# Hybrid S5 and sparse-attention layer on one core: modulation and gate rows on TensorE, attention from unsplit q and k with its division moved to the product with v, elementwise stages in place in PSUM

## The chip, the cores and the metric

The kernel runs on one core of one Trainium2 chip. Its time is the device time of one execution in microseconds. The engines are TensorE (PE, matmuls; PEld is its weight load), VectorE (DVE), ScalarE (ACT), GpSimd (POOL) and SyncE (SP, which issues the DMAs here). Each takes its instructions strictly in the order in which the program gives them, and waits on semaphores for the others.

## What is computed

One layer for a sequence of 512 tokens of width 1024:

```
mod = silu(c) @ w_ada + b_ada                    # 3 x 1024: shift, scale, gate
h = rms_norm(x, g) * (1 + scale) + shift
proj = h @ w_in                                  # 1024 x 3656, then split
y_ssm  = s5(u) with a GLU, * silu(z)             # 32 groups x 16 channels, 64 complex states each
score  = sum_h w_idx * relu(q_idx k_idx^T)       # causal; the 128 best keys of each query stay
logits = (rms_norm(q) rms_norm(k)^T) / 8 + bias  # 8 heads x 64, -inf where a key was not picked
y_attn = (softmax(logits) @ v) * silu(z')
x = x + gate * (concat(y_ssm, y_attn) @ w_out)
```

## The kernel before

Nothing in this kernel is issued where it is written. `record` writes every operation into a list, under a stage name and with the engines that could do it; `Plan.schedule` then makes one order for each engine, by a table of due times per stage (`STAGES`), of shifts per tile (`SHIFT`), of allowed engines (`ONLY`) and by estimated costs (`_cost`). Line 418 issues all of them, so every row of the profile has that line, and tiles are told apart by name. SBUF tiles come from pools of numbered slots (`SLOTS`: 65 of 512 columns, 4 for raw weights, 8 for their converted halves) and PSUM from 8 banks of 128 x 512 fp32.

The large products are split: a weight `wr` is copied to fp32r `wh` and the remainder becomes `wl` (helpers `hi`, `lo`); the same for the activations, and `mm3` adds three fp32r matmuls.

What the change touches, in program order:

- **Modulation** (stages mod0 to mod4, five blocks of 1, 1, 2, 2, 2 groups of 128 channels). The row `modrow` = silu(c) @ w_ada comes for blocks 0 and 1 from matmuls into `pm` (the vector, padded to 32 columns, `cpad`, is the stationary operand, and the eight parts of the sum go to four groups of 32 output rows), and for the blocks in `SIDE` = (2, 3, 4) from VectorE, which multiplies each loaded `wa` (128 x 512) by one column of `cpad` and adds: eight instructions for a block. Then come `Ac`, `Bc`, `hf`, `hh`, `hl`, and the matmuls `pi` of the first 640 columns of w_in.
- **Indexer and top-k** (rel, topk). For each of three query tiles and eight heads two matmuls into `pr`, a relu into `rl`, a multiply-add into `acc`; then 16 rounds of max and match_replace for three tiles (`m`, `work`), which give `mask1` to `mask3`.
- **SSM** (`ssm_quad`, four times). Two PSUM tiles `pd` are copied to `Dt`; six elementwise products and sums, two scans, and six more on 128 x 512, on VectorE or GpSimd, lead to `Xr`, `Xi`, then the matmuls `py` and 16 Gelu pieces `zt`.
- **Projections** (`pp`, 128 x 512, 24 matmuls each).
- **Attention** (at0 to at3, two heads each, four query tiles of widths 128 to 512). `pbx` spreads the norms, `qk` is scaled, and q and k are split into `qs`, `ks`, `kl` (ten half-height operations for each head pair). Logits `pl` come from two fp32r matmuls; bias `G` plus mask is added on VectorE or GpSimd into `lg`; a custom reduction adds `pl` and finds the minimum `nm`; ScalarE takes exp with a running sum; the reciprocal `rc` of the sum scales `lg` (`scaled_half`); transposes go to `ppt`, copies to `pT`, and products with v to `po`.
- **GLU** (`pgl`, `tg`, `ys`), **gate row** (gate: `wag` is w_ada's last third, multiplied and added on VectorE into `gacc`, 16 instructions; then `grow_h`, `grow_l`, `pgb`, `gb`), **output** (`pout`, 9 tiles; times `gb`, plus `xr`, stored from `oo`).

## Time and profile before

| | us |
|---|---|
| three runs | 374.39, 375.29, 380.01 (median 375.29) |
| the profiled execution | 374.05, of it span of the trace 372.2 |
| busy in the span: PE, DVE, ACT, POOL | 330.1, 318.9, 201.0, 139.3 |

Matmuls overlap their neighbours' ends, so a PE that is shown busy is not a PE at its peak; the distance from one start to the next is what a matmul costs in a stream. A group's "idle before" is the idle time of its engine just ahead of its instructions, with what ended it.

### The profile page before, as it was taken

To read this page: it belongs to the slowest core of one execution; us is meant where nothing else is said; L and a number is where in the kernel's file an instruction comes from. 1 tells how busy PE (TensorE), PEld (TensorE's weight loads), DVE (VectorE), ACT (ScalarE), POOL (GpSimd) and SP (SyncE) were. 2 spreads that over 40 slices of the span, in tenths; PEclk is the share of its full clock that TensorE was granted. 3 is DMA by queue.
4 is the path that set the end of the run, shared out by engine and by line. 5 is a ranking of instruction groups with operands and counts; after the bars stand their busy time and mean duration, and the time that the engine had idled before them with its cause. 6 is when DMAs were issued, how large, how long until landed. Compare 5 with 4: busy or idle time off the path is not lost.

```text
span 372.2 us, 5895 instructions
## 1 busy us (share of the span) xinstructions
PE 330.1 (89%) x1934; PEld 268.6 (72%) x1935; DVE 318.9 (86%) x752; ACT 201.0 (54%) x484; POOL 139.3 (37%) x178
## 2 busy tenths in 40 slices
...
GB/s 220 322 311 284 274 137 150 93 57 115 113 2 71 60 29 122 76 17 156 55 3 100 74 272 122 0 56 115 0 110 170 7 111 112 144 2 184 284 113 127
DMA packets 48718, 44.38 MB, mean 119 GB/s; under 512 B 8728, under 2 KB 39784, under 8 KB 48688
## 3 DMA queue, kind: packets, MB, share of 16 engines
...
q8 instruction: 15, 0.25, 0.3%
...
## 4 chain that ended last, share of the span: by engine, by line
DVE 44%; PE 34%; DMA 7%; issue 6%; ACT 5%; POOL 1%; SPq 1%; DVEq 0%; POOLq 0%
PE pp L418 8%; PE pout L418 7%; DVE work L418 6%; PE pi L418 6%; DVE m L418 5%; DVE Dt L418 4%; DVE wl L418 3%; PE pgl L418 3%; DVE acc L418 3%; PE ppt L418 3%; PE po L418 3%; DVE lg L418 3%; DMA wag<-in_w_ada_dram 2%; DVE st L418 2%; DMA wa<-in_w_ada_dram 2%
## 5 line engine op out<-in xcount | busy, mean ns | idle before, releaser
L418 PE MATMUL pp<-hh,wh 128*128 128x512 f32 x152 | 60.8, 404 | 0.0
L418 PE MATMUL pp<-hl,wh 128*128 128x512 f32 x152 | 60.2, 400 | 0.0
L418 PE MATMUL pp<-hh,wl 128*128 128x512 f32 x152 | 59.0, 402 | 1.1 <-DVE wl L418 1.1
L418 ACT ACTIVATE wh<-wr 128x1024 fp32r<-128x1024 f32 (+1 forms) x32 | 30.7, 985 | 17.7 <-PE pp L418 9.3
L418 PEld LDWEIGHTS pp<-hh,wl 128*128 128x128 f32 x152 | 29.0, 191 | 9.0 <-DVE wl L418 2.8
L418 DVE TENSOR_TENSOR wl<-wr,wh 128x1024 fp32r<-128x1024 f32 (+1 forms) x29 | 33.2, 1158 | 2.4 <-PE pi L418 2.2
L418 PEld LDWEIGHTS pp<-hl,wh 128*128 128x128 f32 x152 | 29.4, 194 | 5.7
L418 PEld LDWEIGHTS pp<-hh,wh 128*128 128x128 f32 x152 | 29.4, 193 | 5.5
L418 POOL TENSOR_TENSOR wl<-wr,wh 128x1024 fp32r<-128x1024 f32 (+1 forms) x10 | 23.1, 2323 | 22.6 <-DMA wa<-in_w_ada_dram 11.8
L418 PE MATMUL pout<-wl,yh 128*128 128x512 f32 (+1 forms) x72 | 26.1, 372 | 0.0
L418 PE MATMUL pout<-wh,yh 128*128 128x512 f32 (+1 forms) x72 | 25.9, 375 | 0.0
L418 PE MATMUL pout<-wh,yl 128*128 128x512 f32 (+1 forms) x72 | 25.6, 372 | 0.0
L418 DVE MATCH_REPLACE8 work<-m,work 128x256 f32<-128x256 f32 (+2 forms) x45 | 24.7, 560 | 0.0
L418 DVE MAX8 m<-work 128x8 f32<-128x256 f32 (+2 forms) x45 | 24.0, 565 | 0.0
L418 POOL TENSOR_SCALAR lg<-lg,rc 128x128 f32<-128x128 f32 (+3 forms) x26 | 16.5, 642 | 14.8 <-DVE rc L418 14.5
L418 POOL TENSOR_TENSOR lg<-G,mask 128x256 f32<-128x256 f32 (+1 forms) x6 | 11.7, 1944 | 26.5 <-DVE Dt L418 17.7
L418 ACT ACTIVATE zt<-py 32x128 f32<-32x128 f32 x64 | 17.2, 270 | 7.6 <-PE py L418 6.9
L418 DVE SCALAR_TENSOR_TENSOR modrow<-wa,cpad,modrow 128x512 f32<-128x512 f32 x21 | 16.9, 803 | 3.2 <-DMA wa<-in_w_ada_dram 2.9
L418 PE MATMUL pi<-hh,wh 128*128 128x384 f32 (+2 forms) x50 | 14.0, 347 | 5.0 <-DVE hh L418 5.0
L418 PE MATMUL ppt<-ident,lg 128*128 128x128 f32 x80 | 14.0, 284 | 4.3 <-POOL lg L418 3.2
L418 ACT ACTIVATE lg<-lg,nm 128x128 f32<-128x128 f32 (+3 forms) x32 | 17.7, 554 | 0.1
L418 ACT ACTIVATE T<-Kt 32x64 f32<-32x64 f32 (+3 forms) x61 | 16.5, 270 | 1.7 <-DVE Kt L418 0.9
...
## 6 DMA issues: line engine op xcount, KB each, us to landing
...
```

Of the source, the lines that this page charges most:

```text
L418: getattr(engines[eng], method)(*[val(a) for a in args], **{k: val(a) for k, a in kw.items()})
```

## The change

Five things are done, and the whole order is planned anew.

- `SIDE` is empty: all five blocks' modulation rows are fp32 matmuls into `pm` (24 more, 32 x 512). The gate row is made in the same way (16 matmuls into `pmg`) and copied from PSUM; `gacc` and its 16 instructions are gone.
- q and k are no longer split: `qs`, `ks`, `kl` are gone, and the logits are one fp32 matmul for a head, of its 64 rows, the two heads in turn. For tiles 1 to 3 a matmul of a bf16 identity with the mask starts the sum, so that G plus mask is no longer computed.
- The division by the sum is taken from `lg`: one reciprocal for a head pair, spread to `rcx`, transposed into `prc`, multiplied with the gate into `szr`, which then multiplies `po`. The products with v alternate between the two heads.
- The SSM's twelve elementwise steps and two scans, the relu of the indexer, the GLU's tanh and first product, and the output's product with the gate write into the PSUM tile that they read, on VectorE or ScalarE; the copies to `Dt` are gone.
- `STAGES`, `ONLY`, `SHIFT`, `KEEP`, `WINDOW` and some entries of `_cost` are other numbers, which sets another order on all engines.

```diff
--- before.py
+++ after.py
@@ -439,127 +443,127 @@
-KEEP = {"t2": 9, "raw": 7, "ws": 26, "w2": 29, "psum": 0, "m8": 109}
-WINDOW = 215.7
+KEEP = {"t2": 0, "raw": 22, "ws": 104, "w2": 76, "psum": 0, "m8": 0}
+WINDOW = 269.1
...
-SIDE = (2, 3, 4)
+SIDE = ()
...
-    "const": (-130.13, 19.52), "warm": (160.42, 0.78), "x0": (-53.41, 7.11), "x1": (-225.23, 40.92),
+    "const": (-261.19, 1.5), "warm": (-377.6, 85.79), "x0": (-721.29, 806.27), "x1": (-331.32, 41.75),
...
@@ -620,10 +624,6 @@
...
-    def scaled_half(v, s):
-        P.record([("DVE", "tensor_scalar", (v, v, s, 0.5), dict(op0=ALU.mult, op1=ALU.mult)),
-                  ("POOL", "tensor_scalar", (v, v, s, 0.5), dict(op0=ALU.mult, op1=ALU.mult))])
@@ -642,6 +642,8 @@
...
+    identb = small("identb", [128, 128], BF16)
+    V.tensor_copy(identb, ident)
@@ -1115,32 +1117,31 @@
...
-            d_ = t2("Dt", shape=Q)
-            evac(d_.rearrange("p a b -> p (a b)"), pd)
-            Dt.append(d_)
+            Dt.append(pd.rearrange("p (m n) -> p m n", m=4))
...
            ones_n.unsqueeze(1).to_broadcast(list(Q)))
-        tt(ALU.mult, ta, Dt[1], sn_)
-        tt(ALU.mult, tb_, Dt[0], sn_)
-        tt(ALU.mult, Dt[0], Dt[0], cs_)
-        tt(ALU.mult, Dt[1], Dt[1], cs_)
-        tt(ALU.add, ta, ta, Dt[0])
-        tt(ALU.subtract, tb_, Dt[1], tb_)
+
         Sr, Si = Dt
+        V.tensor_mul(ta, Si, sn_)
+        V.tensor_mul(tb_, Sr, sn_)
+        V.tensor_mul(Sr, Sr, cs_)
+        V.tensor_mul(Si, Si, cs_)
+        V.tensor_add(Sr, Sr, ta)
+        V.tensor_sub(Si, Si, tb_)
         fl = lambda t_: t_.rearrange("p m n -> p (m n)")
-        V.tensor_tensor_scan(fl(Sr), fl(dec), fl(ta), 0.0, ALU.mult, ALU.add)
-        V.tensor_tensor_scan(fl(Si), fl(dec), fl(tb_), 0.0, ALU.mult, ALU.add)
+        V.tensor_tensor_scan(fl(Sr), fl(dec), fl(Sr), 0.0, ALU.mult, ALU.add)
+        V.tensor_tensor_scan(fl(Si), fl(dec), fl(Si), 0.0, ALU.mult, ALU.add)
         Xr, Xi = t2("Xr", shape=Q), t2("Xi", shape=Q)
         G.memset(Xr[:, :, 0:1], 0.0)
         G.memset(Xi[:, :, 0:1], 0.0)
-        tt(ALU.mult, ta, Si, sn_)
-        tt(ALU.mult, tb_, Sr, sn_)
-        tt(ALU.mult, Sr, Sr, cs_)
-        tt(ALU.mult, Si, Si, cs_)
-        tt(ALU.subtract, Xr[:, :, 1:128], Sr[:, :, 0:127], ta[:, :, 0:127])
-        tt(ALU.add, Xi[:, :, 1:128], Si[:, :, 0:127], tb_[:, :, 0:127])
+        V.tensor_mul(ta, Si, sn_)
+        V.tensor_mul(tb_, Sr, sn_)
...
@@ -1226,9 +1227,9 @@
                 pr = bank("pr")
                 T.matmul(pr[:, :W], qix[h][:, ti * 128:(ti + 1) * 128], KH[:, :W], start=True, stop=False)
                 T.matmul(pr[:, :W], qix[h][:, ti * 128:(ti + 1) * 128], KL[:, :W], start=False, stop=True)
-                rl = t2("rl")
-                P.record([("ACT", "activation", (rl[:, :W], pr[:, :W], AF.Relu), {}),
-                          ("DVE", "tensor_scalar", (rl[:, :W], pr[:, :W], 0.0, None), dict(op0=ALU.max))])
+                rl = pr
+                P.record([("ACT", "activation", (pr[:, :W], pr[:, :W], AF.Relu), {}),
+                          ("DVE", "tensor_scalar", (pr[:, :W], pr[:, :W], 0.0, None), dict(op0=ALU.max))])
                 if h == 0:
                     V.tensor_scalar(acc[ti][:, :W], rl[:, :W], wcol[:, ti, 0:1], None, op0=ALU.mult)
                 else:
@@ -1323,18 +1324,6 @@
             V.scalar_tensor_tensor(t, t, gains[:, s_:s_ + 1], pbx, op0=ALU.mult, op1=ALU.mult)
             nrm.append(t)
         qn, kn = nrm
-        kl = t2("kl", F32R, parts=True)
-        for h in range(2):
-            r = slice(64 * h, 64 * h + 64)
-            o = slice(64 - 64 * h, 128 - 64 * h)
-            qs[h], ks_[h] = t2(f"qs{h}", F32R, parts=True), t2(f"ks{h}", F32R, parts=True)
-            hi(qs[h][r], qn[r])
-            lo(qs[h][o], qn[r], qs[h][r])
-            hi(ks_[h][r], kn[r])
-            hi(ks_[h][o], kn[r])
-        for h in range(2):
-            r = slice(64 * h, 64 * h + 64)
-            lo(kl[r], kn[r], ks_[h][r])
         Gt = []
         for h in range(2):
             g, hd = t2(f"G{h}", parts=True), 2 * i + h
@@ -1343,24 +1332,23 @@
             N.dma_start(g[:, 256:512], bskew.raw((128, 256), lambda t, hd=hd: bass.AP(
                 tensor=t.tensor, offset=t.offset + hd * 128 * 385 + 127, ap=[[384, 128], [1, 256]])))
             Gt.append(g)
-        sums, rc = small(f"sums{i}", [128, 4, 2], parts=True), small(f"rc{i}", [128, 4, 2], parts=True)
-        po = bank("po")
+        sums, rc = small(f"sums{i}", [128, 4, 2], parts=True), small(f"rc{i}", [128, 4, 2])
+        po, szr = bank("po"), t2(f"szr{i}")
         for ti in range(4):
             W = 128 * (ti + 1)
             ts_, pTs = slice(ti * 128, ti * 128 + 128), []
-            for h in range(2):
-                r, hd = slice(64 * h, 64 * h + 64), 2 * i + h
-                pl = bank("pl")
-                T.matmul(pl[:, :W], qs[h][:, ts_], ks_[h][:, :W], start=True, stop=False)
-                T.matmul(pl[:, :W], qs[h][r, ts_], kl[r, :W], start=False, stop=True)
-                lg, nm, g = t2("lg"), P.tile("m8", "nm", [128, 1], F32), Gt[h][:, 512 - W:512]
-                if ti:
-                    tt(ALU.add, lg[:, :W], g, masks[ti][:, :W])
-                    g = lg[:, :W]
-                V.tensor_tensor_reduce(lg[:, :W], pl[:, :W], g, 1.0, 3e38, ALU.add, ALU.min, nm)
+            pls = [bank("pl") for _ in range(2)]
+
+            for pl in pls if ti else ():
+                T.matmul(pl[:, :W], identb, masks[ti][:, :W], start=True, stop=False)
+            with P.together():
+                for h, pl in enumerate(pls):
+                    r = slice(64 * h, 64 * h + 64)
+                    T.matmul(pl[:, :W], qn[r, ts_], kn[r, :W], start=(ti == 0), stop=True)
+            for h, pl in enumerate(pls):
+                lg, nm = t2("lg"), P.tile("m8", "nm", [128, 1], F32)
+                V.tensor_tensor_reduce(lg[:, :W], pl[:, :W], Gt[h][:, 512 - W:512], 1.0, 3e38, ALU.add, ALU.min, nm)
                 S.activation(lg[:, :W], lg[:, :W], AF.Exp, scale=-1.0, bias=nm, accum_out=sums[:, ti, h:h + 1])
-                V.reciprocal(rc[:, ti, h:h + 1], sums[:, ti, h:h + 1])
-                scaled_half(lg[:, :W], rc[:, ti, h:h + 1])
                 pp = bank("ppt")
                 for sj in range(ti + 1):
                     T.transpose(pp[:, sj * 128:(sj + 1) * 128], lg[:, sj * 128:(sj + 1) * 128], ident)
@@ -1368,21 +1356,28 @@
                 evac(pT[:, :W], pp[:, :W])
                 pTs.append(pT)
             with P.together():
-                for h, pT in enumerate(pTs):
-                    r, hd = slice(64 * h, 64 * h + 64), 2 * i + h
-                    for sj in range(ti + 1):
+                for sj in range(ti + 1):
+                    for h, pT in enumerate(pTs):
+                        r, hd = slice(64 * h, 64 * h + 64), 2 * i + h
                         c0 = (sj % 2) * 256 + (hd % 4) * 64
                         T.matmul(po[r, ts_], v_t[hd // 4, sj // 2][:, c0:c0 + 64],
                                  pT[:, sj * 128:(sj + 1) * 128], start=(sj == 0), stop=(sj == ti),
                                  skip_group_check=True)
-        po_[i] = po
+
+        V.reciprocal(rc, sums)
+        rcx, prc = t2("rcx", shape=(128, 4, 2, 64)), bank("prc")
+        scaled(rcx, 0.5, rc.unsqueeze(3).to_broadcast([128, 4, 2, 64]))
+        for ti in range(4):
+            T.transpose(prc[:, ti * 128:(ti + 1) * 128], rcx[:, ti].rearrange("p h d -> p (h d)"), ident)
+        V.tensor_mul(szr, prc, szt[2560 + 128 * i])
+        po_[i] = po, szr
     def attn_out(i):
         stage(f"ao{i}")
-        po = po_[i]
+        po, szr = po_[i]
         y = t2("ya")
         V.tensor_mul(y.rearrange("c (j p) -> c p j", j=4), po.rearrange("c (p j) -> c p j", j=4),
-                     szt[2560 + 128 * i].rearrange("c (p j) -> c p j", j=4))
+                     szr.rearrange("c (p j) -> c p j", j=4))
         split_y(4 + i, y)
@@ -1409,10 +1404,10 @@
...
-            th_, y = t2("tg"), t2("ys")
-            S.activation(th_, p, AF.Tanh, scale=0.5, bias=hbglu[:, o:o + 1])
-            V.scalar_tensor_tensor(th_, th_, 1.0, zt_q[o], op0=ALU.add, op1=ALU.mult)
-            V.scalar_tensor_tensor(y.rearrange("c (j p) -> c j p", j=4), th_.rearrange("c (j p) -> c j p", j=4),
+            y = t2("ys")
+            S.activation(p, p, AF.Tanh, scale=0.5, bias=hbglu[:, o:o + 1])
+            V.scalar_tensor_tensor(p, p, 1.0, zt_q[o], op0=ALU.add, op1=ALU.mult)
+            V.scalar_tensor_tensor(y.rearrange("c (j p) -> c j p", j=4), p.rearrange("c (j p) -> c j p", j=4),
                                    0.25, szt[512 + 128 * o].rearrange("c (p j) -> c j p", j=4),
@@ -1425,19 +1420,17 @@
         for hf in range(2):
             brg = t2("brg")
             N.dma_start(brg, a["b_ada"][0:1, 2048 + 512 * hf:2560 + 512 * hf].to_broadcast([128, 512]))
-            acc = t2("gacc")
+            pmg = bank("pmg")
             for kk in range(NK):
                 if kk % 2 == 0:
                     wa = P.tile("raw", "wag", [128, 2, 512], F32)
                     N.dma_start(wa, w_ada[:, kk:kk + 2, 2048 + 512 * hf:2560 + 512 * hf])
-                ck = cpad[:, kk, 0:1]
-                if kk == 0:
-                    V.tensor_scalar(acc, wa[:, 0], ck, None, op0=ALU.mult)
-                else:
-                    V.scalar_tensor_tensor(acc, wa[:, kk % 2], ck, acc, op0=ALU.mult, op1=ALU.add)
+                g = kk % 4
+                T.matmul(pmg[32 * g:32 * g + 32], cpad[:, kk, :], wa[:, kk % 2], start=(kk < 4), stop=(kk >= 4))
+
             rh, rl, pgb, gb = t2("grow_h", F32R), t2("grow_l", F32R), bank("pgb"), t2(f"gb{hf}")
-            hi(rh, acc)
-            lo(rl, acc, rh)
+            evac(rh, pmg)
+            V.tensor_sub(rl, pmg, f(rh))
             T.matmul(pgb, onesc, rh, start=True, stop=False)
             T.matmul(pgb, onesc, rl, start=False, stop=True)
             V.tensor_add(gb, pgb, brg)
@@ -1496,8 +1489,8 @@
                     wh, wl = ws[k // 2]
                     mm3(p[:, 0:w], y_hi[k][:, js], y_lo[k][:, js], wh[:, k % 2, cs_], wl[:, k % 2, cs_], n == 0, n == 7)
                 o = t2("oo")
-                V.tensor_mul(o[:, 0:w], p[:, 0:w], gateb[hf][:, cs_])
-                tt(ALU.add, o[:, 0:w], o[:, 0:w], xr[:, cs_])
+                V.tensor_mul(p[:, 0:w], p[:, 0:w], gateb[hf][:, cs_])
+                V.tensor_add(o[:, 0:w], p[:, 0:w], xr[:, cs_])
                 N.dma_start(outv[:, j, hf * 512 + c0:hf * 512 + c0 + w], o[:, 0:w])
```

Where the order moves, at three places. PE, in the program's last third, where attention begins (`pbx` of the first head pairs; `pp` are the last projections). Before:

```order
L418 MATMUL pbx_2924<-rT_2920,sel_201 128x512
L418 MATMUL pbx_2926<-rT_2920,sel_201 128x512
L418 MATMUL pbx_2928<-rT_2920,sel_201 128x512
L418 MATMUL pbx_2930<-rT_2920,sel_201 128x512
L418 MATMUL pp_2917<-hh_127_511,wl_642_2922 128x512
L418 MATMUL pp_2917<-hh_155_608,wh_637_2907 128x512
```

The same place of the change (`identb` is the identity, the operands of the last two rows are q and k of one pair):

```order
L422 MATMUL pbx_2952<-rT_2863,sel_143 128x512
L422 LDWEIGHTS identb_118
L422 MATMUL pl_2955<-mask_611_2937,identb_118 128x256
L422 LDWEIGHTS identb_118
L422 MATMUL pl_2958<-mask_611_2937,identb_118 128x256
...
L422 MATMUL pl_2955<-qk_421_1966,qk_417_1931 128x256
L422 MATMUL pl_2958<-qk_421_1966,qk_417_1931 128x256
```

Before, 66 matmuls of `pp` stand behind the first `pbx`, mixed with the first logits; in the change none does: all projections are ahead of it. The gate row, before on DVE at the program's end, between the output's products:

```order
L418 SCALAR_TENSOR_TENSOR gacc_4005<-wag_4001,cpad_80,gacc_4005 128x512
L418 TENSOR_TENSOR gb_937_4036<-pgb_4030,brg_3349 128x512
L418 SCALAR_TENSOR_TENSOR gacc_4005<-wag_4001,cpad_80,gacc_4005 128x512
L418 TENSOR_TENSOR oo_4045<-pout_3694,gb_937_4036 128x512
L418 TENSOR_TENSOR oo_4049<-pout_3699,gb_937_4036 128x512
```

In the change on PE, in attention, eight in a row, the second half some 100 matmuls later in the same way:

```order
L422 MATMUL pl_3123<-qk_573_2700,qk_576_2713 128x512
L422 MATMUL pmg_3176<-wag_3149,cpad_99 32x512 x2
L422 MATMUL pmg_3176<-wag_3151,cpad_99 32x512 x2
L422 MATMUL pmg_3176<-wag_3153,cpad_99 32x512 x2
L422 MATMUL pmg_3176<-wag_3155,cpad_99 32x512 x2
L422 MATMUL pbx_3203<-rT_2863,sel_143 128x512
```

The gate row leaves the last output products, and its matmuls now stand ahead of attention's. ACT, in the change, where attention begins (`zt` are the last pieces of an SSM's Gelu, `lg` the exponentials; a table load stands where the function needs another table):

```order
L422 ACT_TABLE_LOAD
L422 ACTIVATE zt_613_2941<-py_2876 32x128
L422 ACT_TABLE_LOAD
L422 ACTIVATE lg_3059,sums_665_3067<-lg_3059,nm_3060 128x256
L422 ACTIVATE lg_3064,sums_665_3067<-lg_3064,nm_3065 128x256
```

Before, the last `zt` all stood ahead of the first exponential; now three of them stand between exponentials, with five table loads where one was. In the whole program ACT has 17 loads, and had 10.

## Rows read from the trace of the kernel before

**Rows 1.** The page's first part: busy time, share of the span and instructions of each engine.

```profile
span 372.2 us, 5895 instructions
PE 330.1 (89%) x1934; PEld 268.6 (72%) x1935; DVE 318.9 (86%) x752; ACT 201.0 (54%) x484; POOL 139.3 (37%) x178
```

**Rows 2.** Three stretches of the span: up to the first round of the top-k, from there to the first `pbx` of attention, and the rest. The columns stand in the first row.

```profile
core 0: us, PE busy (x) PEld busy (x) DVE busy (x) ACT busy (x) POOL busy (x), PEclk, DMA share, GB/s
0.00:118.50 118.50, 101.51 (x628) 86.94 (x630) 98.10 (x262) 61.09 (x145) 27.17 (x59) 0.93 0.57 163
118.50:247.40 128.90, 112.43 (x662) 91.62 (x661) 121.49 (x270) 86.57 (x220) 65.33 (x69) 0.99 0.30 84
247.40:372.20 124.80, 116.18 (x646) 90.08 (x646) 99.36 (x222) 53.31 (x120) 46.85 (x51) 0.97 0.35 114
```

**Rows 3.** What PE's matmuls waited for in the whole span: us in total, times, longest.

```profile
PE py L418 <- DVE Xr L418: 5.9, 2, 5.1
PE pi L418 <- DVE hh L418: 5.0, 1, 5.0
PE ppt L418 <- POOL lg L418: 3.2, 2, 2.3
...
PE pbx L418 <- ACT rT L418: 2.8, 1, 2.8
...
PE ppt L418 <- DVE rc L418: 0.9, 2, 0.7
```

**Rows 4.** The groups of instructions of DVE, forms kept apart: the modulation and gate rows (busy us, mean ns | idle before).

```profile
L418 DVE SCALAR_TENSOR_TENSOR modrow<-wa,cpad,modrow 128x512 f32<-128x512 f32 x21 | 16.9, 803 | 3.2 <-DMA wa<-in_w_ada_dram 2.9
L418 DVE SCALAR_TENSOR_TENSOR gacc<-wag,cpad,gacc 128x512 f32<-128x512 f32 x14 | 11.3, 804 | 1.3 <-DMA wag<-in_w_ada_dram 1.1
```

**Rows 5.** PE in order of time (start us, us, form, matmul records): fp32 matmuls with 32 stationary columns. Each fp32 matmul leaves two records. First four matmuls of 256 columns on four groups of output rows, and what started behind them, then the window's busy times with the granted clock; then two matmuls of 512 columns on one and the same group.

```profile
23.58 1.08 PE L418 MATMUL pm<-wa,cpad 128*32 128x256 f32 x8 [1.09 <-DMA wa<-in_w_ada_dram]
24.59 0.48 PE L418 MATMUL px<-ident,x 128*128 128x128 f32 x1
...
23.50:24.60 1.10, 1.02 (x9) 0.24 (x9) 0.00 (x0) 0.00 (x0) 0.00 (x0) 0.50 0.98 318
...
162.88 2.24 PE L418 MATMUL psq<-sq,blk 128*32 128x512 f32 x4
162.80:165.00 2.20, 2.05 (x6) 0.28 (x4) 2.20 (x5) 2.14 (x8) 0.91 (x1) 1.00 0.02 4
```

**Rows 6.** Groups of DVE and POOL in attention, forms kept apart.

```profile
L418 DVE TENSOR_TENSOR lg<-G,mask 128x512 f32<-128x512 f32 x8 | 5.7, 742 | 0.0
L418 DVE TENSOR_TENSOR lg<-G,mask 128x384 f32<-128x384 f32 x7 | 3.7, 557 | 0.6 <-PE pp L418 0.6
L418 DVE TENSOR_TENSOR lg<-G,mask 128x256 f32<-128x256 f32 x3 | 1.2, 416 | 0.0
L418 DVE RECIPROCAL rc<-sums 128x1 f32<-128x1 f32 x32 | 5.1, 161 | 6.2 <-ACT lg L418 6.0
L418 DVE TENSOR_TENSOR qs<-qk,qs 64x512 fp32r<-64x512 f32 x7 | 5.1, 739 | 0.2
L418 DVE TENSOR_TENSOR kl<-qk,ks 64x512 fp32r<-64x512 f32 x7 | 4.8, 691 | 0.2
```

**Rows 7.** PE in order of time at four places of attention: the spacing of `pp`; two `kl` of 384 columns and one of 512 (64 rows each, in the window from 271.45); all eight logit matmuls of one head, and the next transposes; ten products with v (two records each) and what started behind them.

```profile
265.00 0.39 PE L418 MATMUL pp<-hh,wh 128*128 128x512 f32 x1
265.22 0.39 PE L418 MATMUL pp<-hl,wh 128*128 128x512 f32 x1
265.45 0.39 PE L418 MATMUL pp<-hh,wl 128*128 128x512 f32 x1
...
271.51 0.68 PE L418 MATMUL pl<-kl,qs 64*128 64x384 f32 x3
...
284.26 0.91 PE L418 MATMUL pl<-ks,qs 128*128 128x128 f32 x4
285.10 0.90 PE L418 MATMUL pl<-kl,qs 64*128 64x128 f32 x4
285.93 0.44 PE L418 MATMUL ppt<-ident,lg 128*128 128x128 f32 x2
...
288.42 1.58 PE L418 MATMUL po<-pT,v 128*64 128x128 f32 x20
289.93 0.49 PE L418 MATMUL pbx<-rT,sel 32*128 32x512 f32 x1
```

**Rows 8.** Groups of DVE and POOL whose 128 x 512 operands lie in SBUF or in PSUM.

```profile
L418 DVE TENSOR_TENSOR Dt<-Dt,cos 128x512 f32<-128x512 f32 x13 | 8.6, 702 | 0.0
L418 POOL TENSOR_TENSOR Dt<-Dt,cos 128x512 f32<-128x512 f32 x3 | 3.9, 1290 | 0.1
L418 DVE TENSOR_TENSOR oo<-pout,gb 128x512 f32<-128x512 f32 x7 | 4.4, 683 | 0.0
L418 DVE TENSOR_TENSOR ya<-po,sz 128x512 f32<-128x512 f32 x4 | 4.3, 1080 | 1.7 <-PE po L418 1.7
```

**Rows 9.** Groups of ACT: the exponentials, the read of their sum, table loads.

```profile
L418 ACT ACTIVATE lg<-lg,nm 128x128 f32<-128x128 f32 (+3 forms) x32 | 17.7, 554 | 0.1
L418 ACT ACTIVATION_READ_ACCUMULATOR lg<-lg,nm 128x1 f32 x32 | 6.1, 191 | 0.0
L418 ACT ACT_TABLE_LOAD x10 | 12.8, 1283 | 1.0 <-PEq L1539 0.8
```

More of the change, by code (lines that the diff above doesn't have):

```diff
@@ L140, in _cost @@
         aps = sum(isinstance(kw.get(k), View) for k in ("scale", "bias"))
+        if out.shape[0] == 32 and out.base.shape[0] > 32:
+            return 225 + 93 * aps + 0.45 * n
         return (51 if ps else 93) + 93 * aps + 0.833 * n + (93 if "accum_out" in kw else 0)
@@ L150, in _cost @@
             return 140 + 0.85 * n
-        return 148 + (1.667 if all(v.spread for v in args[1:3]) else 2.1) * n
+        return 170 + (1.667 if all(v.spread for v in args[1:3]) else 2.1) * n
     return 50
```

29 lines of the change are left out of this document (16 added, 13 removed), and 197 rows, old and new, of tables (ONLY, SHIFT, STAGES).

## The prediction

> **What bounds the kernel now.** I read the page's first part, then three stretches of the span, then what PE waited for, then the groups and PE's order of time at the places that the change touches. The first part shows two engines near the top: PE 330.1 and DVE 318.9 of 372.2 us [rows 1]. No single engine is the bound, so the stretches matter. Up to the top-k's first round (118.5 us) DVE is busy for 98.1 and PE for 101.5; the rest is start and DMA (share 0.57). From there to attention DVE is the bound, 121.5 of 128.9, and PE has 16.5 idle. In the last 124.8 us PE is the bound, 116.2, with 8.6 idle, and DVE has 25.4 free [rows 2]. PE's longest waits outside attention are for DVE: 5.9 for Xr, 5.0 for hh; 2.8 for rT is ACT's, behind DVE's norms. In attention they are for the scaled logits, 3.2 behind POOL and 0.9 behind the reciprocal [rows 3].
>
> So work taken from DVE pays in the first two stretches until PE binds, and work added to PE costs in the last, unless it fills its waits.
>
> **Prices on PE.** In a stream a 512-column fp32r matmul starts every 0.228 us (265.00 to 265.45) [rows 7]. For fp32 with 32 stationary columns there are two ends. Four of 256 columns on four row groups took 1.01 us (23.58 to 24.59) at a granted clock of 0.50, the lower of the two levels, 1.2 GHz; at 2.4 GHz that is 0.505, and at 512 columns 1.01 for four, 0.25 each. Two of 512 columns on one group took 2.24, so 1.1 each [rows 5]. In the new order the 40 new ones stand in runs on alternating groups, as the four did, so I take 0.25: 24 for the modulation are 6.0 (at the other end 26), 16 for the gate 4.0 (18).
>
> **Up to the top-k.** DVE loses the 21 modrow steps, 16.9 us [rows 4]. The new order puts about 6 us of small copies and squares on it in exchange, so it is shorter by 11: 98.1 becomes 87, and with the same waits the top-k starts at 107.5. PE pays 6.0 there, but has 17.0 idle, and the wait of 5.0 for hh falls on the chain that is removed, so it is no later. What is late next is the landing of w_ada and then the weights of `pv`; the DMAs are the same bytes in another order. Ends: 2 us gained, if the loads set this stretch, and 17, if nothing comes in exchange.
>
> **From the top-k to attention.** DVE: 11 of the bias-plus-mask sums stand in this stretch, 4 x 0.742 + 4 x 0.557 + 3 x 0.416 = 6.4 [rows 6]. GpSimd did 10 of the SSM's elementwise steps, at 1.29; in PSUM all are VectorE's, at 0.70: +7.0. The trace has no step that reads and writes PSUM on DVE; a read from PSUM costs 0.683 against 0.702 from SBUF, and the dearest such row is 1.080, with a strided order [rows 8]. I take 0.70, since the order of elements is plain; 64 steps at 1.08 would be 24 us, the upper end. The copies to Dt go, the tables shift a little to GpSimd: -3 in all, and DVE needs 118.5 with its idle 7.4 on top, 125.9, to 233.4.
> PE now also has the 66 `pp` in this stretch that stood behind the first `pbx`: 66 x 0.228 = 15.0. 112.4 + 15.0 = 127.4, which is more than DVE's, so PE binds: 107.5 + 127.4 = 234.9, and with 4 of waits (0 to 16.5, as before) 238.9 where attention begins, against 247.4.
>
> **From attention to the end**, on PE, from 116.2:
> - the 66 `pp` are done: -15.0; the gate row: +4.0; 16 transposes of the reciprocals, at the 0.15 of a product with v at most (ten from 288.42 to 289.93) [rows 7]: +2;
> - logits: a head took 1.67 (284.26 to 285.93), eight heads 13.4. Now 1,280 fp32 columns a head at about 2.0 ns (0.505 us for 256) are 2.5 alone, 1.3 if the two heads' row halves run side by side, and the mask adds 1,152 columns, 0.51: 14.2 to 24.4 for eight. Two `kl` of 384 columns on the two halves took 0.28, since of the 0.68 for three the last lasts 0.40, where one after the other is 0.34 [rows 7]; they do overlap, and fp32 streams longer behind the same weight load. I take +2, ends +1 and +11;
> - the products with v alternate between the heads, so that each stands beside one on the other half: 80 x 0.151 = 12.1, of which I take 3 off (0 to 6).
> That is 106.2. Of the idle 8.6 the 4.1 behind POOL's and DVE's scaling go [rows 3]. The cover goes too: the `pp` filled PE while the first logits went through DVE and ACT. ACT has five table loads there where one was, 4 x 1.283 more [rows 9], ahead of exponentials for which the transposes wait: +5. So 106.2 + 9.5 = 115.7.
> DVE loses 11.3 of gacc, 5.1 of reciprocals, 9.9 of q and k parts and 4.2 of sums here [rows 4, 6]; as it was free for 25.4 this pays nothing by itself, but the end no longer waits for it.
>
> **The sum.** 238.9 + 115.7 = 354.6 of span against 372.2, 17.6 less. The profiled execution took 374.05, 1.85 around its span, and stands 1.24 below the median of 375.29. I take the difference from the median: 357.7, 358.
>
> Changes of tile form on PE: the logits of a head are 2,560 columns, 1.14 at 0.228, and took 1.67 with two changes between 128 and 64 rows, so a change costs up to 0.26 [rows 7]. Counted over the whole order there are 55 such changes before and 36 after, up to 5 us less; the sum leaves that out, since the 1.67 holds it for the logits already, and it stands among the rivals. The Trainium skill, TensorEngine Tiling, Key Properties, says that changing the tiling mode, not just the tile, drains the engine, which would speak against 40 new narrow matmuls; the row agrees that a change costs something, and the order holds fewer of them, so that by the page, too, the change comes out lower and not higher.
>
> **Rivals.**
> - PE keeps its waits. Every engine's order is fixed, DVE is as full as before between top-k and attention, and the SSM's PSUM tiles are now held through scans and products, of 8 banks. If PE idles for 16.5 there again, it is 12.5 more: 370, no change. For it: the 5.9 for Xr. Against it: 11 us less of DVE before.
> - fp32 side by side fails. If each new narrow matmul takes 1.1 and the two heads go in turn, PE pays 20 in the first stretch (half of it in idle time), 14 for the gate row and 9 for the logits: 33 more, 391. Against it: the four in 1.01.
> - On the other side, one place: attention without cover. ACT has exponentials 17.7 and sum reads 6.1 [rows 9], most copies to pT by the new order (about 11), and some 12 of table loads, tanh and conversions: 47 to 52 us. If PE's transposes and products stand behind this chain in turn instead of beside it, the stretch grows from 115.7 by up to 37: 395, slower. It decides from 25 us of extra waits on. For it: the trace shows that already with `pp` as cover transposes waited 4.1. Against it: logits of the next pair stand ahead in PE's order, and the GLU's 48 matmuls (11 us) stand between.
> - Fewer changes of tile form: 19 fewer at up to 0.26 are 5 less, 353. For it: the runs of eight and the half-height operands that go. Against it: changes that fall into waits cost nothing now.
>
> **How the numbers follow.** The forecast, 358, gets 0.52, and fewer changes of form, 353, gets 0.20; both lie in their common own range, 344 to 367. PE keeping its waits, 370, gets 0.17; fp32 in turn 0.05; attention without cover 0.06. A measurement of this kernel tells about 2% from no change, so the lines are 367.8 and 382.8. Faster is 0.72, same 0.17, slower 0.11. The range for 8 in 10 goes from 344 (17 instead of 11 us in the first stretch, no waits in the second, 6 off the products with v) to 376 (370 and half of the logits' upper end); the two slow cases stay outside.
>
> **What would show it.** In the changed profile: top-k's first `m` near 107 us, and `pbx` near 239. DVE's busy total near 275 (318.9 less 11, 3 and 30) and PE's 330 to 345. Runs of `pm` and `pmg` of eight with about 2 us each; `pd<-pd` products near 0.70 us; pairs of `pl<-qk` that start together. Wrong would be: `py` or `pp` waiting for DVE for more than 15 us in the middle stretch, the start of top-k unmoved (then the loads set it), `ppt` waiting for ACT's lg for more than 15 us, or `pd` steps above 1 us.

## The result and the profile after

The changed kernel takes 362.42 us (median of four runs, 361.80 to 362.77). The ratio to the kernel before is 0.969, 95% interval 0.963 to 0.975: faster by 3.1%. The forecast was 358, with a range from 344 to 376. From here on every median, lowest and highest is of fast runs, those not more than 1.5% above the fastest of their kernel; mod_alone's two slow runs, 396.6 and 398.2, would lift its median from 389.5 to 393.4.

The profiled execution took 362.77, its span 361.1. The first part of the page, to be laid beside [rows 1]:

```profile
span 361.1 us, 5955 instructions
PE 333.5 (92%) x2055; PEld 271.4 (75%) x2055; DVE 275.8 (76%) x662; ACT 178.1 (49%) x424; POOL 124.6 (35%) x175
```

TensorE has 3.4 us more work than before and 27.6 idle instead of 42.1. That is the whole gain: 14.5 less idle, 3.4 more work, 11.1 of span. VectorE lost 43 and is no longer near the top.

The same three stretches as [rows 2], cut at the same two events, the first round of the top-k (114.1 us) and the first `pbx` (250.9):

```profile
core 0: us, PE busy (x) PEld busy (x) DVE busy (x) ACT busy (x) POOL busy (x), PEclk, DMA share, GB/s
0.00:114.10 114.10, 101.14 (x688) 87.67 (x689) 88.74 (x258) 52.68 (x110) 36.62 (x78) 0.93 0.59 171
114.10:250.90 136.80, 131.05 (x719) 108.13 (x717) 122.36 (x263) 76.49 (x189) 74.05 (x88) 0.99 0.33 93
250.90:361.10 110.20, 101.31 (x653) 75.59 (x652) 64.68 (x144) 48.90 (x125) 13.96 (x10) 1.00 0.32 110
```

| stretch | before | forecast | after |
|---|---|---|---|
| to the top-k | 118.5 | 107.5 | 114.1 |
| to attention | 128.9 | 131.4 | 136.8 |
| to the end | 124.8 | 115.7 | 110.2 |

The first two came out 6.6 and 5.4 longer than forecast, the last 5.5 shorter. What TensorE waited for longest (beside [rows 3]; the waits for `Xr`, `hh` and the scaled logits are gone; those for `w` and `qi`, in the middle and the first stretch, are new; the one for `blk`, at the program's start, was 3.2):

```profile
PE pd L422 <- DVE w L422: 4.6, 1, 4.6
PE psel L422 <- DVE blk L422: 4.6, 1, 4.6
PE pr L422 <- DVE qi L422: 4.4, 1, 4.4
...
PE ppt L422 <- ACT lg L422: 1.0, 2, 0.8
```

The wait of `pr` stands at 92 us. Three pieces of the order of time around it, of TensorE, VectorE and GpSimd (start us, us, form):

```profile
96.43 0.55 PE L422 MATMUL pr<-KH,qi 128*128 128x256 f32 x1 [4.42 <-DVE qi L422]
...
88.92 6.23 DVE L422 TENSOR_TENSOR w<-cwo,cwt 64x320 f32<-64x320 f32 x4
95.16 1.12 DVE L422 TENSOR_TENSOR qi<-pi,qi 64x384 fp32r<-64x384 f32 x2
...
88.58 5.22 POOL L422 TENSOR_TENSOR wl<-wr,wh 128x1024 fp32r<-128x1024 f32 x2 [0.34 <-ACT wh L422]
```

The four `w` steps take 6.23; the other four of the kernel take 1.9 together (the group of eight is 8.1 in the groups of VectorE). They began while GpSimd made two `wl`, 5.22 us, and `qi`, for which TensorE waits, stands behind them in VectorE's order. What TensorE's clock did then (the stretches before the wait, the wait, what came behind it; the columns are those of the windows above):

```profile
86.00:92.00 6.00, 5.43 (x39) 4.70 (x37) 5.99 (x6) 5.82 (x12) 4.54 (x3) 1.00 0.33 87
92.00:96.40 4.40, 0.01 (x1) 0.00 (x0) 4.31 (x6) 0.73 (x3) 1.80 (x1) 0.93 0.76 202
96.40:102.40 6.00, 5.97 (x27) 6.00 (x28) 4.26 (x8) 2.60 (x8) 0.00 (x0) 0.50 0.10 30
102.40:108.00 5.60, 5.60 (x37) 5.42 (x37) 4.82 (x11) 4.25 (x10) 1.76 (x2) 0.98 0.00 0
```

After 4.4 us of idling the granted clock is 0.50, the lower level of 1.2 GHz, for 6.0 us in which TensorE is full: 3.0 us of work are lost on top of the wait.

The prices that the sum used, in the groups of TensorE and VectorE after (busy us, mean ns) and, in order of time, one run of eight `pmg`:

```profile
L422 PE MATMUL po<-pT,v 128*64 128x128 f32 x160 | 9.8, 276 | 0.0
L422 PE MATMUL psq<-sq,blk 128*32 128x512 f32 x16 | 2.3, 597 | 0.0
...
L422 PE MATMUL pmg<-wag,cpad 128*32 128x512 f32 x32 | 3.8, 598 | 0.0
L422 DVE TENSOR_TENSOR pd<-pd,cos 128x512 f32<-128x512 f32 x16 | 10.4, 688 | 0.0
...
267.66 1.92 PE L422 MATMUL pmg<-wag,cpad 128*32 128x512 f32 x16
```

Eight fp32 matmuls (two records each) take 1.92, 0.24 each, where 0.25 was forecast; a `pd` step in PSUM takes 0.688, where 0.70 was. The same groups before for the first two lines:

```profile
L418 PE MATMUL po<-pT,v 128*64 128x128 f32 x160 | 14.0, 280 | 0.1
L418 PE MATMUL psq<-sq,blk 128*32 128x512 f32 x16 | 5.0, 599 | 0.4 <-ACT sq L418 0.3
```

### The profile page after: what moved, and what is told of

The parts are those of the page before. It is cut to its first block, busy times and chain, and to the rows that moved or that the text cites. A ratio compares the mean times of both kernels' runs of the same rounds, so it can differ in the third digit from the quotient of the medians.

```text
span 361.1 us, 5955 instructions
## 1 busy us (share of the span) xinstructions
PE 333.5 (92%) x2055; PEld 271.4 (75%) x2055; DVE 275.8 (76%) x662; ACT 178.1 (49%) x424; POOL 124.6 (35%) x175
## 4 chain that ended last, share of the span: by engine, by line
PE 54%; DVE 14%; ACT 11%; DMA 7%; issue 6%; POOL 5%; SPq 3%; DVEq 0%; POOLq 0%; ACTq 0%
PE pp L422 18%; PE pout L422 12%; PE pi L422 7%; DMA wa<-in_w_ada_dram 4%; ACT lg L422 4%; PE pv L422 4%; PE pr L422 3%; SPq L422 3%; PE pd L422 2%; DVE wl L422 2%; DVE work L422 2%; DVE m L422 2%; ACT L422 2%; PE pt L422 2%; PE pm L422 2%
## 5 line engine op out<-in xcount | busy, mean ns | idle before, releaser
L422 PE MATMUL pp<-hh,wh 128*128 128x512 f32 x152 | 59.5, 394 | 0.0
L422 POOL TENSOR_TENSOR wl<-wr,wh 128x1024 fp32r<-128x1024 f32 x15 | 38.9, 2605 | 50.6 <-ACT wh L422 33.9
L422 DVE TENSOR_TENSOR wl<-wr,wh 128x1024 fp32r<-128x1024 f32 (+1 forms) x24 | 28.4, 1208 | 19.5 <-ACT wh L422 17.6
L422 ACT ACTIVATE wh<-wr 128x1024 fp32r<-128x1024 f32 (+1 forms) x25 | 24.8, 1017 | 34.5 <-PE pout L422 16.7
L422 POOL TENSOR_SCALAR wh<-wr 128x1024 fp32r<-128x1024 f32 (+1 forms) x11 | 10.3, 936 | 39.4 <-DMA wr<-in_w_in_dram 30.0
L422 ACT ACTIVATE lg<-lg,nm 128x256 f32<-128x256 f32 (+3 forms) x32 | 17.6, 552 | 8.1 <-DVE nm L422 8.1
L422 ACT ACTIVATE sq<-pp 128x512 f32<-128x512 f32 x8 | 4.8, 599 | 24.9 <-PE pp L422 8.1
L422 ACT ACTIVATE U<-pp 32x128 f32<-32x128 f32 x47 | 12.6, 269 | 9.0 <-PE pp L422 8.4
L422 PE MATMUL pi<-hl,wh 128*128 128x384 f32 (+2 forms) x50 | 17.0, 351 | 0.0
L422 PE MATMUL pi<-hh,wl 128*128 128x384 f32 (+2 forms) x50 | 16.7, 350 | 0.2 <-DVE wl L422 0.2
```

What stands on the lines that cost most here:

```text
L422: getattr(engines[eng], method)(*[val(a) for a in args], **{k: val(a) for k, a in kw.items()})
```

## The experiments

In all of them the instructions of one of the two kernels keep their order on each engine, their engine and, as far as tiles live as long, their buffers: the order that the planner had made is written out as a list. What an edit replaces stands where the replaced instruction stood. So no time below holds a new plan. The changed kernel with its order written out and no other edit was not run; topk_12, at 362.9, shows no price of writing it out. The kernel before had medians from 372.1 to 374.9 beside them.

| run | us (median, lowest to highest) | ratio to before, 95% |
|---|---|---|
| the changed kernel | 362.4, 361.8 to 362.8 | 0.969, 0.963 to 0.975 |
| undo_mod | 372.0, 370.4 to 374.1 | 0.996, 0.992 to 1.000 |
| undo_gate | 372.8, 370.2 to 374.4 | 1.000, 0.995 to 1.006 |
| undo_div | 379.0, 374.6 to 379.7 | 1.014, 1.004 to 1.025 |
| undo_logits | 389.7, 389.0 to 390.2 | 1.045, 1.040 to 1.050 |
| gate_one_group | 370.7, 368.5 to 372.5 | 0.991, 0.986 to 0.995 |
| topk_12 | 362.9, 359.9 to 364.0 | 0.970, 0.963 to 0.978 |
| z_two_products | 359.4, 358.8 to 360.2 | 0.962, 0.958 to 0.967 |
| joint | 359.7, 358.7 to 360.7 | 0.965, 0.958 to 0.971 |
| move_both | 359.2, 357.1 to 361.1 | 0.964, 0.957 to 0.971 |
| move_and_fill | 356.5, 354.5 to 357.9 | 0.957, 0.950 to 0.963 |
| mod_alone | 389.5, 388.8 and 390.2 | 1.045, 1.034 to 1.056 |
| mod_alone_runs | 374.0, 372.3 to 377.1 | 1.001, 0.997 to 1.006 |

### One part undone in the changed kernel

**undo_mod.**

```diff
-SIDE = ()
+SIDE = (2, 3, 4)
```

> The changed kernel with the modulation rows of blocks 2 to 4 back on VectorE (21 scalar_tensor_tensor, three scaled copies), each step at the place in the order where its matmul stood; every other instruction keeps its engine and its place. Theory A (TensorE sets the time: its work plus its own gaps): TensorE loses 24 matmuls, about 6, VectorE has 25 idle of the first 114 us to take 16.9 more; the wait for hh comes back, 5.0 before, with a stretch of low clock behind it. Net -5 to +5, so 357 to 367. Theory B (VectorE's busy time sets the first stretch, as the first step of the prediction had it): +11 to +17, 373 to 379.

372.0, 9.6 more: between the two ranges, nearer to VectorE's. TensorE waits 6.7 for `modrow` and 5.4 for a landing of `wa`, and what follows is 8 to 10 us later (the first `acc` at 108.4 instead of 98.7, attention at 258.7 instead of 250.9). Theory A was too low: as the wait for `modrow` shows, the 25 idle us of VectorE did not all lie where the row is needed.

**undo_gate.**

```diff
-                T.matmul(pmg[32 * g:32 * g + 32], cpad[:, kk, :], wa[:, kk % 2], start=(kk < 4), stop=(kk >= 4))
+                    V.scalar_tensor_tensor(acc, wa[:, kk % 2], ck, acc, op0=ALU.mult, op1=ALU.add)
```

> The changed kernel with the gate row back on VectorE (16 steps over 128x512), each at the place of its matmul, everything else in place. Theory A: TensorE loses 16 matmuls, 3.7, and VectorE has 45 idle in the last 110 us, so 358 to 363. Theory B (what is taken from VectorE pays by itself): +11.3, 371 to 375.

372.8, as theory B had it, but not by its reason. VectorE is busy for 79.1 of the last 125.3 us. The rows of VectorE and TensorE in order of time show where most of the price is:

```profile
295.88 3.89 DVE L266 SCALAR_TENSOR_TENSOR gacc<-wag,cpad,gacc 128x512 f32<-128x512 f32 x5
299.69 0.20 DVE L266 RECIPROCAL rc<-sums 128x8 f32<-128x8 f32 x1
...
301.09 1.11 PE L266 MATMUL prc<-ident,rcx 128*128 128x128 f32 x4 [6.10 <-POOL rcx L266]
...
294.60:301.00 6.40, 0.39 (x2) 0.00 (x0) 6.22 (x13) 2.66 (x9) 0.95 (x1) 0.67 0.37 97
301.00:312.00 11.00, 10.91 (x80) 9.07 (x80) 9.04 (x11) 6.44 (x11) 4.66 (x4) 0.72 0.49 179
```

Five `gacc` stand ahead of the reciprocal of which `prc` is made; TensorE stands for 6.1 and then runs at a granted clock of 0.72 (third column from the right). In the changed kernel the wait for `rcx` is 1.2. The wait and the lower clock make 4.9 and 3.1 of the 10.4 us. So here work on an engine with 46 us to spare costs its place, not its length.

**undo_div.**

```diff
+                V.reciprocal(rc[:, ti, h:h + 1], sums[:, ti, h:h + 1])
+                P.record([("DVE", "tensor_scalar", (lg[:, :W], lg[:, :W], rc[:, ti, h:h + 1], 0.5), ...
-        scaled(rcx, 0.5, rc.unsqueeze(3).to_broadcast([128, 4, 2, 64]))
```

> The changed kernel with the probabilities divided again before their transposes (a reciprocal and a scaling for each of 32 tiles, on the engines that did them before), without the 16 transposes of the reciprocals. Theory A: TensorE loses 1.9 and waits for the scaling as in the kernel before, about 4: 362 to 367. Rival (no projection is left to cover these waits): each of the 16 pairs of tiles waits 1 us more, 376 to 380.

379.0, 16.6 more: the rival, by its size. TensorE's transposes wait for the scaled logits and for VectorE, which is late:

```profile
PE ppt L266 <- POOL lg L266: 5.2, 4, 2.5
...
PE ppt L266 <- DVE nm L266: 3.6, 3, 1.9
```

In the changed kernel `ppt` waits 1.0 for ScalarE and 0.2 for VectorE. The mean granted clock of the span is 0.939 instead of 0.972.

**undo_logits.**

```diff
-            for pl in pls if ti else ():
-                T.matmul(pl[:, :W], identb, masks[ti][:, :W], start=True, stop=False)
-                    T.matmul(pl[:, :W], qn[r, ts_], kn[r, :W], start=(ti == 0), stop=True)
+                T.matmul(pl[:, :W], qs[h][:, ts_], ks_[h][:, :W], start=True, stop=False)
+                T.matmul(pl[:, :W], qs[h][r, ts_], kl[r, :W], start=False, stop=True)
...
+                    tt(ALU.add, lg[:, :W], g, masks[ti][:, :W])
```

> The changed kernel with q and k split again into high and low parts, two fp32r matmuls a head, and the mask added on VectorE and GpSimd; the rest in place, division on the product with v kept. Theory A: TensorE's logits go from 16.5 back to 13.6, and the parts stand ahead of a pair's first logits for some 4 us: 360 to 368. Rival (this part carries the gain): the parts and sums, 14.1 on VectorE alone, land on the path: 372 or more.

389.7, 27 more; the rival, and by more than it asked. TensorE waits 7.5 for `qs`, 3.1 for `ks`, and 5.4 instead of 4.6 for `w`, at a mean clock of 0.920.

Each undone part costs from 9.6 to 27 us, 64 together, while the whole change gives 12. These numbers are therefore no shares of the gain: an order made for one content has no room for another. The elementwise steps in PSUM were not undone alone; what they bring stays open.

### What a narrow fp32 matmul costs

**gate_one_group.**

```diff
-                T.matmul(pmg[32 * g:32 * g + 32], cpad[:, kk, :], wa[:, kk % 2], start=(kk < 4), stop=(kk >= 4))
+                T.matmul(pmg[0:32], cpad[:, kk, :], wa[:, kk % 2], start=(kk == 0), stop=(kk == 7))
```

> The changed kernel with the 16 matmuls of the gate row all on one group of 32 columns instead of in turn on four (its sum is then one row, so the copies and the broadcast behind it read 32 partitions). In the changed kernel four of 512 columns take two passes of 0.43, 0.215 each. Theory A (side by side is what makes them cheap, and TensorE's time counts): each takes 0.86, 13.7 instead of 3.7, so +8 to +14, 370 to 376. Rival (they overlap anyway, or lie in waits): 362 to 365.

370.7, theory A. Eight take 7.05 us instead of 1.92, 0.88 each instead of 0.24; the group, 14.1 instead of 3.8, carries 10.3 of which 8.3 reach the end:

```profile
265.34 7.05 PE L266 MATMUL pmg<-wag,cpad 128*32 128x512 f32 x16
```

**mod_alone** and **mod_alone_runs**, in the kernel before.

```diff
-SIDE = (2, 3, 4)
+SIDE = ()
```

> The kernel before with one part of the change alone: the modulation rows of blocks 2 to 4 on TensorE (24 matmuls and three copies on ScalarE where 21 steps of VectorE and three scaled copies stood), every other instruction in its place. Theory B (VectorE's 16.9 set the first stretch): -11 to -17, 358 to 364. Theory A (only the wait of 5.0 for hh goes, and the low clock behind it, 5 us at half speed): 366 to 370. Rival (an order made for other work gives the time back at the next wait): 372 to 376.

389.5, some 16 more than before: every theory missed. Each matmul stands where its VectorE step had stood, one by one among the matmuls `pi`:

```profile
40.10 1.05 PE L262 MATMUL pm<-wa,cpad 128*32 128x512 f32 x2
41.08 0.38 PE L262 MATMUL pi<-hh,wl 128*128 128x256 f32 x1
...
L262 PE MATMUL pm<-wa,cpad 128*32 128x512 f32 x48 | 26.0, 624 | 0.0
```

One alone holds TensorE for 0.98 to the next start; the 24 take 26.0, all ahead of 72 us, where the granted clock is 1.00. The same 24 with the eight of a block one behind the other:

> As mod_alone, but the eight matmuls of each of the blocks 2 to 4 stand one behind the other in TensorE's order, where the last VectorE step of the block stood; every other instruction of the kernel before is in its place. In mod_alone the 24 stood singly between matmuls of pi, each holding TensorE for about 1.2 (40.10 to 41.08 for its two passes, some 0.2 more around them), 28 us in all, against 0.215 in the changed kernel's runs. Theory G (the price is set by whether they stand together): 24 x 0.97 less than mod_alone's 393, so 366 to 372, and by what VectorE is relieved of no more than that. Theory B (VectorE's 16.9 also count): 356 to 364. Rival (the place in the order costs, not the form): 385 to 393.

374.0, the time of the kernel before, 15.5 less than one by one. The group of all 24, and one block in order of time:

```profile
L262 PE MATMUL pm<-wa,cpad 128*32 128x512 f32 x48 | 5.8, 598 | 0.0
...
40.49 1.92 PE L262 MATMUL pm<-wa,cpad 128*32 128x512 f32 x16
```

26.0 against 5.8 are 20.2 us, of which 16.3 reach the top-k's start (116.9 against 133.2 in mod_alone) and 15.5 the end. Theory G had the mechanism, and its 366 to 372 missed by 2; theory B is refuted here: with 16.9 us of VectorE taken away and TensorE's wait for `hh` gone, the top-k starts at 116.9 instead of 118.5 and the end does not move. By itself this part gives nothing in the order of before; in the changed order the same part undone costs 9.6.

### What holds the middle stretch

**topk_12**, **z_two_products** and **joint**, in the changed kernel.

```diff
-        for r in range(16):
+        for r in range(12):
...
+        if P.stage[0] != "z":
-        T.matmul(o, lh, rl, start=False, stop=False)
+            T.matmul(o, lh, rl, start=False, stop=False)
```

> The changed kernel with 12 rounds of the top-k instead of 16 (it leaves out 24 steps of VectorE, about 13 us, so that 96 and not 128 keys are kept a row); order otherwise unchanged. Theory A: 360 to 362.5, only the wait at 189.8 us stands behind the top-k. Theory B: -13, 349.

> The changed kernel without the product of the weights' high part with h's low part in seven of the z projections (it leaves out 56 matmuls of 0.228 us, 12.8 of TensorE); order otherwise unchanged. Theory A: TensorE's time counts one to one until VectorE binds, which is busy for 122.4 of the 136.8 us between top-k and attention: 350 to 352. Theory B: less than 3 off, 359 to 363.

> The changed kernel with both cuts of the runs topk_12 and z_two_products at once (it leaves out 24 steps of the top-k, 13 us of VectorE, and 56 matmuls, 12.8 us of TensorE). Alone the first gave nothing and the second 3. Theory D (the middle stretch is held by VectorE and TensorE together, either is there when the other is relieved): 347 to 351. Theory E (a third chain holds it, the steps of the SSM's tables over GpSimd, ScalarE and VectorE between 148 and 195 us): 357 to 360, as the second cut alone.

362.9, 359.4 and 359.7. (The first is 0.4 above its theory A.) Without 13 us of VectorE nothing moves, which refutes theory B; without 12.8 of TensorE 3.0 are gained, which refutes theory A; without both no more is gained, as theory E had it. The middle stretch of z_two_products holds 119.8 of TensorE in 133.1 us, and the chain of work in joint says on what it hangs (start us, us, what):

```profile
172.19 13.33 DMA wr<-in_w_in_dram
...
185.68 1.05 POOL wh L266
186.72 0.72 POOL cwo L266
...
190.78 0.86 POOL w L266
191.70 0.87 POOL w L266
192.59 0.70 DVE w L266
193.30 0.14 issue
193.43 0.76 PE pd L266 x2
```

A load of weights lands at 185.5, GpSimd converts it (`wh`) and then makes a table's `w` in seven more steps; when the last ends, VectorE may copy `ptw`, and `pd` starts. It starts at 193.4 here, at 193.0 in z_two_products, at 194.4 in topk_12 and at 194.85 in the changed kernel, whatever TensorE and VectorE were relieved of. In topk_12 VectorE stands idle ahead of that copy (in the changed kernel and in z_two_products it does not: there the copy stands behind steps of the top-k, and comes about 1 us after GpSimd's last `w`):

```profile
193.57 0.69 DVE L266 COPY w<-ptw 128x512 f32<-128x512 f32 x1 [3.45 <-POOL w L266]
```

### The two waits moved

**move_both.** Rows of VectorE's order, nothing else is touched:

```diff
-w<-cwo,cwt x4
 qi<-pi,qi x2
 KL<-pk,KH
 qi<-pi,qi x2
+w<-cwo,cwt x4
...
+w<-ptw
 work<-m,work (and five more steps of the top-k)
-w<-ptw
```

> The changed kernel with eleven VectorE instructions moved and nothing else: the qi subtractions and KL ahead of the four w steps of the first table (which stood behind GpSimd's wl for 2.67 and 2.55 us instead of 0.49), and one copy of w from ptw ahead of six steps of the top-k. Theory A: TensorE's two longest waits go, 4.4 at 91.7 and 4.6 at 189.8, and with the first the stretch of low clock behind it, 2 to 3: 350 to 354. Rival: the next wait in the chain stands in their place, 358 to 363.

359.2 in the median, in the rival's range and not in theory A's; the profiled execution, 357.14, is the fastest of the four and has a span of 355.4. The stretches, and the clock where the wait stood:

```profile
0.00:108.30 108.30, 97.37 (x688) 82.24 (x689) 84.65 (x258) 52.45 (x110) 36.82 (x78) 0.97 0.62 180
108.30:245.20 136.90, 131.58 (x717) 107.92 (x715) 121.15 (x263) 76.38 (x189) 73.66 (x87) 0.99 0.32 93
245.20:355.40 110.20, 101.39 (x653) 75.61 (x652) 64.71 (x145) 48.95 (x125) 13.94 (x10) 0.99 0.33 110
...
93.00:95.20 2.20, 0.22 (x3) 0.07 (x1) 2.01 (x5) 0.74 (x3) 0.00 (x0) 1.00 0.80 219
95.20:102.00 6.80, 6.80 (x44) 6.46 (x45) 6.58 (x14) 4.84 (x11) 1.75 (x2) 1.00 0.10 30
```

Theory A's mechanism holds for the first move and fails for the second. The top-k starts at 108.3 instead of 114.1: TensorE's wait is 2.0 instead of 4.4, and after it the clock stays at 1.00. The middle stretch keeps its 136.9, though `pd` no longer waits: TensorE waits there for `wl` (2.5) and `wh` (2.2) instead. So the table's steps alone do not hold that stretch: with their wait gone, other waits on converted weights take its place, and what would shorten it stays open. One trace of each says little to a microsecond: in eight runs whose order up to the top-k is the changed kernel's own, it starts between 111.5 and 114.8 (113.3 in the mean). The four `w` and the steps ahead of them, beside the same two `wl` of GpSimd:

```profile
88.53 1.14 DVE L266 TENSOR_TENSOR qi<-pi,qi 64x384 fp32r<-64x384 f32 x2 [0.43 <-ACT qi L266]
...
92.18 2.38 DVE L266 TENSOR_TENSOR w<-cwo,cwt 64x320 f32<-64x320 f32 x4
...
87.69 5.03 POOL L266 TENSOR_TENSOR wl<-wr,wh 128x1024 fp32r<-128x1024 f32 x2 [0.34 <-ACT wh L266]
```

`qi`, with one operand in PSUM, takes its 0.56 beside `wl` as elsewhere, and the four `w`, which now begin 0.5 us ahead of the end of `wl`, take 2.4 instead of 6.2.

**move_and_fill.** The first move alone, and sums of zeros in TensorE's idle time between 24 and 30 us (they add nothing):

```diff
+    for i in range(16):
+        T.matmul(p_idx[3], zero[:, 0:128], zero, start=False, stop=False)
```

> The changed kernel with the qi subtractions and KL ahead of the four w steps (as in move_both, without the move of the copy from ptw) and with 16 matmuls by a tile of zeros, 128x512, added into the sums of pi3 at three places where TensorE stands idle between 24 and 30 us. In the changed kernel the granted clock is 0.50 from 27.3 to 37.4 us after that idle time, and TensorE is full there. Theory F (the clock's 5 us are on the path): 352 to 356. Rival (the loads, whose queues are full until 46 us, set that stretch): 357 to 360.

356.5, between theory F's range and the rival's. The clock from 28.0 to 37.4 us, in the changed kernel and here:

```profile
28.00:37.40 9.40, 9.40 (x47) 8.46 (x48) 7.32 (x31) 2.78 (x5) 0.83 (x1) 0.50 0.94 296
...
28.00:37.40 9.40, 9.40 (x77) 7.41 (x78) 8.43 (x34) 3.44 (x6) 0.83 (x1) 1.00 0.91 286
```

It stays at 1.00, but the first `acc` comes at 94.5, as in move_both (94.6): the 4.7 us of work that the clock gives back were not on the path there. The top-k starts at 109.5 (108.3 in move_both). Only the first attention step is earlier, 243.6 against 245.2. Whether the zeros or the copy left in its place did that, these two runs do not tell. This version is the fastest of all, 0.957 of before; its runs (354.5 to 357.9) lie below all of the changed kernel's (361.8 to 362.8).

## Why the prediction was right, and where its steps missed

**Direction and mechanism.** Faster, by relieving TensorE of waits at a small price in its own work: 14.5 of idle against 3.4 of work. The totals that were named came out: VectorE 275.8 (near 275), TensorE 333.5 (330 to 345), `pd` at 0.688 (0.70), runs of eight at 1.92 (2). None of the four signs of a wrong forecast appeared: no wait of `py` or `pp` over 0.5, `ppt` waits 1.0 for ScalarE, and the top-k's start moved. The two starts that were named did not come out: 114.1 for the top-k (near 107) and 250.9 for attention (near 239).

**What was luck.** The first two stretches missed by 12.0 together, and 5.5 of that came back in the last, partly by what was not in the sum. Without it the time would have been 368, at the line of 367.8 that the prediction drew between faster and same.

**The step that failed: "with the same waits the top-k starts at 107.5".** The waits were not the same. VectorE's work came out as forecast (88.7 against 87), but two of its steps were held by GpSimd, `qi` stood behind them, and TensorE lost 4.4 of waiting and 3.0 of clock. With VectorE's steps in the other order the top-k starts at 108.3 and 109.5 (move_both, move_and_fill), against 113.3 in the mean of the eight traces without it. So some 4 of the 6.6 missing us are this wait, shown by two runs; up to 6 by the single pair of traces. The Trainium skill, SBUF — State Buffer, SBUF: two separate sides, says that VectorE with two SBUF inputs and GpSimd share a pair of ports under an exclusive lock, which the first holds for its whole instruction; the 6.23 us for four `w` beside two `wl`, and 2.38 when most of `wl` was over, agree with it. VectorE's order, known before, had the four `w` ahead of `qi`; that GpSimd would be at two `wl` just then is what no order tells. The step's reason, that VectorE's work sets this stretch, is not borne out either: with the same 16.9 us taken from VectorE in the order of before (mod_alone_runs) the top-k starts 1.6 earlier, not 11; put back in the changed order (undo_mod), it makes the start 9.5 later. That the start without the wait comes within 2 us of 107.5 is in part luck.

**The price of the modulation and the gate, 0.25 each, with 1.1 as the other end.** 0.24 and 0.88 to 0.98 were measured. The step rested on runs of alternating groups in the new order, and that is what carries it: one by one the 24 of the modulation cost 20.2 us more in the order of before, and 15.5 at the end. Here the rival "fp32 side by side fails" had its condition wrong: both prices exist, and the order decides which is paid. The Trainium skill, TensorEngine Tiling, Key Properties, says that different tiles load and multiply independently, and that a change of the tiling mode drains the engine. 0.24 on four groups in turn against 0.88 on one agrees with the first; for the second, 0.98 alone among matmuls of 128 columns against 0.88 in a run leaves 0.10 at most.

**"PE binds" in the middle stretch.** TensorE is full there, 131.1 of 136.8, and yet 12.8 less of it gave 3.0. A full engine was taken for the bound; a chain over a load and GpSimd's table steps ends at about the same time, and with its wait gone (move_both) the stretch is 136.9 as before. What binds it is not shown. That the stretch is 5.4 longer than forecast has two parts: TensorE's content is 131.1 instead of 127.4, because the planner set other work there (`pp` has 157 matmuls more than before in this stretch, where the sum moved 66, and the 86 of `pt` are gone from it), and its idle time 5.75 instead of 4, mostly the one wait of 4.6 for `w`.

**The last stretch, 5.5 better.** TensorE needs 101.3 instead of 106.2. The logits cost 2.8 more than before (17.6 against 14.8 by the windows of `pl` alone; +2 forecast), the products with v 4.2 less (3 forecast), the gate row 3.8 (4.0). Not in the sum: `pgl` takes 11.5 instead of 15.0 (its window alone), in another order around it, which no run separates. The idle time is 8.9 (9.5 forecast), though not by the table loads that were to add 5: transposes wait 1.0 for ScalarE, `pl` 1.7 for `ys`, `prc` 1.2 for `rcx`.

**Fewer changes of form (353, 0.20).** Some of TensorE's groups did get cheaper: `pgl` by 3.5 and `py` from 14.3 to 11.5, and `psq` from 5.0 to 2.3. The last is another effect: its eight narrow fp32 matmuls, one group of 32 columns for each pair, now stand in one run, as those of the gate row do. That fewer changes of form made the other two cheaper is not shown. These 9 us lie in the same sum as the waits above, and the net is 362.

**The rivals.** "Attention without cover" did not occur, but its mechanism is real: with the scaling back between exponential and transposes `ppt` waits 8.8, and undoing this part costs 16.6 in all. "PE keeps its waits" (370) was half right in kind: not the old waits, two new ones, 9.0 together.
